# Sliding windows copied by DMA alone: 84 groups of 16 blocks through SBUF instead of 88, and direct copies of 32 rows instead of 16

## The chip, the core and the metric

The kernel runs on one core of a Trainium2 chip. No compute engine does any work in it: the data is moved by the core's 16 DMA engines, which are fed from two queues. SyncE (SP) issues the DMAs of one queue, ScalarE (ACT) those of the other. The metric is the device time of one execution in microseconds. Before the change the median of five runs is 760.02 us (757.92 to 760.73). The profile is of one execution that took 760.15 us.

## The reference

```python
x = randn(32, 4096, 256) float32           # batch, length, dim
window_size, stride = 64, 32
n_windows = (4096 - 64) // 32 + 1          # 127
for i in range(n_windows):
    result[:, i] = x[:, i * 32 : i * 32 + 64]
```

Nothing is computed; rows are copied. The length is cut into 128 blocks of 32 rows by 256 floats, 32 KB a block. Window i of a batch is blocks i and i+1, 64 KB in one piece, both in the input and in the output. Every block but the first and the last of a batch therefore lands in the output twice: as the first half of window i and as the second half of window i-1. The input has 134.2 MB, the output 266.3 MB.

## The kernel before

The batches are divided between two ways of copying, and the two run side by side from the first microsecond.

*Direct* (class `Direct`, issued by SP, line 45): batches 0 to 20. A DMA copies windows from the input in HBM to the output in HBM. A row of such a DMA is one window, 64 KB; the input is read at a step of one block, so that it is read twice over. The 127 windows of a batch take seven DMAs of 16 rows and one of 15. The argument `max_dma_last_dim` cuts a row into pieces: four of 16 KB in the DMAs of 16 rows, two of 32 KB in the DMA of 15 rows. That makes 147 DMAs of 16 rows (1024 KB) and 21 of 15 rows (960 KB). SP waits for nothing before it issues one.

*Staged* (class `Staged`, issued by ACT): batches 21 to 31. A group is 16 neighbouring blocks of a batch, 8 groups a batch, 88 in all. A group is loaded to SBUF once (line 79, 16 rows of 32 KB, cut in two pieces of 16 KB) and stored twice (line 91): once as first halves of windows (`half` 0), once as second halves (`half` 1). The first group of a batch has no second half for its first block, and the last group no first half for its last block, so that 22 of the 176 stores have 15 rows. There are 24 slots in SBUF for groups (6 tiles with 4 slots each). ACT loads 10 groups first (`LEAD`), and then in turn a group ten ahead and the two stores of a group. A store waits for its own load (`loaded`), a load into a slot that has been used waits for the two stores that read it (`stored`).

The order in each queue is thus the program's order. A DMA's pieces are given to the 16 engines by rows, and each engine that takes part ends its share of the DMA with a small write of 4 bytes that counts up a semaphore. Each engine has both queues before it. Every direct DMA and the stores of the last 24 groups count on the semaphore `done`, and SP waits for its full count at the end.

Of the kernel before, what the change touches and what calls it, by code (L numbers as in the profile page):

```python
# [1 line left out]

# [4 lines left out]


DIRECT, STAGE = 16384, 16384
N_STAGED = 11  # L10
N_TILES = 6
LEAD = 10


class Geometry:


    def __init__(self, tc, x, out, B, L, D, W, S, n_win):
        assert W == 2 * S and L % S == 0 and n_win == L // S - 1
        self.x, self.out = x, out  # L20
        self.blk, self.nb, self.nw = S * D, L // S, n_win
        self.done, self.total = tc.alloc_semaphore("done"), 0

    def xap(self, b, block, dims):
        return bass.AP(self.x.tensor, self.x.offset + (b * self.nb + block) * self.blk, dims)

    def oap(self, b, w, half, dims):
        at = ((b * self.nw + w) * 2 + half) * self.blk
        return bass.AP(self.out.tensor, self.out.offset + at, dims)

    def count(self, dma):
        dma.then_inc(self.done, 16)
        self.total += 16


class Direct:


    def __init__(self, g, batches):
        self.g, self.batches = g, batches  # L40

    def windows(self, q, b, w0, n, size):
        g = self.g
        g.count(
            q.dma_start(
                out=g.oap(b, w0, 0, [[2 * g.blk, n], [1, 2 * g.blk]]),
                in_=g.xap(b, w0, [[g.blk, n], [1, 2 * g.blk]]),
                max_dma_last_dim=size,
            )
        )  # L50

    def run(self, q):
        full = self.g.nw // 16 * 16
        for b in self.batches:
            for w0 in range(0, full, 16):
                self.windows(q, b, w0, 16, DIRECT)
            self.windows(q, b, full, self.g.nw - full, 2 * DIRECT)


class Staged:  # L60

    def __init__(self, g, tc, pool, dtype, batches, n_tiles):
        self.g = g
        tiles = [pool.tile([128, g.blk], dtype, name=f"xb{i}") for i in range(n_tiles)]
        self.slots = [t[32 + c : 96 : 4, :] for t in tiles for c in range(4)]
        self.loaded = [tc.alloc_semaphore(f"loaded{i}") for i in range(len(self.slots))]  # L70
        self.stored = [tc.alloc_semaphore(f"stored{i}") for i in range(len(self.slots))]
        self.groups = [(b, j) for b in batches for j in range(0, g.nb, 16)]

    def load(self, q, r):
        g, (b, j) = self.g, self.groups[r]
        n, i = divmod(r, len(self.slots))
        if n:
            q.wait_ge(self.stored[i], 32 * n)
        q.dma_start(
            out=self.slots[i], in_=g.xap(b, j, [[g.blk, 16], [1, g.blk]]),  # L80
            max_dma_last_dim=STAGE,
        ).then_inc(self.loaded[i], 16)

    def store(self, q, r):
        g, (b, j) = self.g, self.groups[r]
        n, i = divmod(r, len(self.slots))
        q.wait_ge(self.loaded[i], 16 * (n + 1))
        for half in (0, 1):
            lo = 1 if half and j == 0 else 0
            hi = 15 if not half and j + 16 == g.nb else 16  # L90
            dma = q.dma_start(
                out=g.oap(b, j + lo - half, half, [[2 * g.blk, hi - lo], [1, g.blk]]),
                in_=self.slots[i][lo:hi, :],
                max_dma_last_dim=STAGE,
            )
            if r + len(self.slots) < len(self.groups):
                dma.then_inc(self.stored[i], 16)
            else:
                g.count(dma)

    def run(self, q, lead):
        for r in range(lead):
            self.load(q, r)
        for r in range(len(self.groups)):
            if r + lead < len(self.groups):
                self.load(q, r + lead)
            self.store(q, r)


@with_exitstack  # L110
def kernel(
    ctx: ExitStack,
    tc: tile.TileContext,
    x: bass.AP,
    window_size: bass.AP,
    stride: bass.AP,
    out: bass.AP,
):
    nc = tc.nc
    W, S = int(window_size), int(stride)  # L120
    B, L, D = x.shape
    n_win = (L - W) // S + 1
    assert out.shape == (B, n_win, W, D)
    g = Geometry(tc, x, out, B, L, D, W, S, n_win)
    pool = ctx.enter_context(tc.tile_pool(name="xb", bufs=1))
    staged = Staged(g, tc, pool, x.dtype, range(B - N_STAGED, B), N_TILES)
    direct = Direct(g, range(B - N_STAGED))
    with tc.tile_critical():
        staged.run(nc.scalar, LEAD)
        direct.run(nc.sync)  # L130
        nc.sync.wait_ge(g.done, g.total)


# [1 line left out]
_INS = ['x', 'window_size', 'stride']  # L135
_OUTS = [((32, 127, 64, 256), 'float32')]

_NUMBERS = {'window_size': 64, 'stride': 32}


# [26 lines left out]
```

## Time and profile before

| what | value |
|---|---|
| median of five runs | 760.02 us (757.92 to 760.73) |
| the profiled execution | 760.15 us |
| its span, from the first to the last instruction | 758.4 us |
| busy compute engines | POOL 0.2 us, none else |
| bytes moved by the DMA engines | 312.53 MB, mean 412 GB/s |
| direct queue (q1, issued by SP) | 12705 packets, 174.80 MB |
| staged queue (q10, issued by ACT) | 12606 packets, 137.71 MB |
| last direct issue begins | 684.8 us |
| last store issue begins | 693.6 us |

A packet is one piece that one DMA engine moves: 16 KB, 32 KB or the 4 bytes of a semaphore. The span is to be read against the DMA rows only. The page's chain that ended last follows instructions of the compute engines, and there are none here. An issue that takes several microseconds is one that had to wait until the queue took it. "Us to landing" is from the issue of a DMA to the arrival of its last byte, and holds the time that it stood in its queue.

### The profile page before, as it was taken

To read this page: it belongs to the slowest core of one execution; us is meant where nothing else is said; L and a number is where in the kernel's file an instruction comes from. 1 tells how busy PE (TensorE), PEld (TensorE's weight loads), DVE (VectorE), ACT (ScalarE), POOL (GpSimd) and SP (SyncE) were. 2 spreads that over 40 slices of the span, in tenths; PEclk is the share of its full clock that TensorE was granted. 3 is DMA by queue.
4 is the path that set the end of the run, shared out by engine and by line. 5 is a ranking of instruction groups with operands and counts; after the bars stand their busy time and mean duration, and the time that the engine had idled before them with its cause. 6 is when DMAs were issued, how large, how long until landed. Compare 5 with 4: busy or idle time off the path is not lost. (4 is left out here: it accounts for less than half of the span.)

```text
span 758.4 us, 482 instructions
## 1 busy us (share of the span) xinstructions
POOL 0.2 (0%) x4
## 2 busy tenths in 40 slices
POOL 0000000000000000000000000000000000000000
DMA  8999999999999999999999999999999999999994
GB/s 365 417 404 412 417 423 418 418 426 419 424 418 425 419 421 423 420 425 420 422 412 427 422 418 418 425 421 423 421 424 413 424 416 423 417 422 414 404 403 200
DMA packets 25314, 312.53 MB, mean 412 GB/s; under 512 B 6869, under 2 KB 6869, under 8 KB 6869
## 3 DMA queue, kind: packets, MB, share of 16 engines
q1 hardware_dynamic: 12705, 174.80, 55.1%
q10 hardware_dynamic: 12606, 137.71, 43.6%
q14 instruction: 3, 0.02, 0.0%
HBM read 220.92 MB, written 266.34 MB: 643 GB/s over the span
## 5 line engine op out<-in xcount | busy, mean ns | idle before, releaser
L148 POOL MEMSET const-bfloat16-1.0<- 128x1 bf16 x1 | 0.1, 101 | 0.0
L148 POOL MEMSET const-uint8-127<- 128x1 uint8 x1 | 0.1, 101 | 0.0
L148 POOL MEMSET const-float32-0.0<- 128x1 f32 x1 | 0.1, 98 | 0.2 <-issue 0.2
L148 POOL MEMSET const-float32-1.0<- 128x1 f32 x1 | 0.1, 98 | 0.0
## 6 DMA issues: line engine op xcount, KB each, us to landing
out_dram<-in_x_dram SPq DMA_DIRECT2D x147, 1024.0 KB, 70.4
out_dram<-xb ACTq DMA_DIRECT2D x154, 512.0 KB, 69.5
xb<-in_x_dram ACTq DMA_DIRECT2D x88, 512.0 KB, 72.3
out_dram<-in_x_dram SPq DMA_DIRECT2D x21, 960.0 KB, 69.6
out_dram<-xb ACTq DMA_DIRECT2D x22, 480.0 KB, 69.8
```

Of the source, the lines that this page charges most:

```text
L148: nc = _bacc.Bacc("TRN2", target_bir_lowering=False, num_devices=1)
```

## The change

Two constants take the place of one: `GROUPS = 84` for `N_STAGED = 11`, and a new `ROWS = 32`. The staged part is now the last 84 groups of all 256: the second half of batch 21 (blocks 64 to 127) and batches 22 to 31. The direct part is everything before: batches 0 to 20, and windows 0 to 63 of batch 21. Direct DMAs take 32 rows as long as 32 are left, then 16, then the rest. A batch of 127 windows takes three DMAs of 32 rows, one of 16 and one of 15; the 64 windows of batch 21 take two of 32. The very first staged group leaves out the second half of its first block, because window 63 is now copied directly.

```diff
-N_STAGED = 11
+GROUPS = 84
+ROWS = 32
@@ class Direct
-    def __init__(self, g, batches):
-        self.g, self.batches = g, batches
+    def __init__(self, g, windows):
+        self.g = g
+        self.parts = [(b, min(g.nw, windows - b * g.nw)) for b in range(-(-windows // g.nw))]
...
     def run(self, q):
-        full = self.g.nw // 16 * 16
-        for b in self.batches:
-            for w0 in range(0, full, 16):
-                self.windows(q, b, w0, 16, DIRECT)
-            self.windows(q, b, full, self.g.nw - full, 2 * DIRECT)
+        for b, n in self.parts:
+            w0 = 0
+            while n - w0 >= 16:
+                m = ROWS if n - w0 >= ROWS else 16
+                self.windows(q, b, w0, m, DIRECT)
+                w0 += m
+            if n > w0:
+                self.windows(q, b, w0, n - w0, 2 * DIRECT)
@@ class Staged
-        self.groups = [(b, j) for b in batches for j in range(0, g.nb, 16)]
+        self.groups = groups
...
-            lo = 1 if half and j == 0 else 0
+            lo = 1 if half and (r == 0 or j == 0) else 0
@@ tile_sliding_window_1d_kernel
-    staged = Staged(g, tc, pool, x.dtype, range(B - N_STAGED, B), N_TILES)
-    direct = Direct(g, range(B - N_STAGED))
+    groups = [(b, j) for b in range(B) for j in range(0, g.nb, 16)][-GROUPS:]
+    staged = Staged(g, tc, pool, x.dtype, groups, N_TILES)
+    b, j = groups[0]
+    direct = Direct(g, b * g.nw + j)
```

More of the change, by code (lines that the diff above doesn't have):

```diff
@@ L52, in run, with __init__ @@
     def run(self, q):
-        full = self.g.nw // 16 * 16
-        for b in self.batches:
-            for w0 in range(0, full, 16):
-                self.windows(q, b, w0, 16, DIRECT)
-            self.windows(q, b, full, self.g.nw - full, 2 * DIRECT)
+        for b, n in self.parts:
[6 more added lines that the diff above has]
+                self.windows(q, b, w0, n - w0, 2 * DIRECT)
 class Staged:
-    def __init__(self, g, tc, pool, dtype, batches, n_tiles):
+    def __init__(self, g, tc, pool, dtype, groups, n_tiles):
         self.g = g
```

## The prediction

> **What bounds the kernel now.** I read the page's DMA rows first, since no compute engine works, then the stretches of the span with their DMA share, then the instructions in order of time, and last the packet records in the trace. The page:
>
> ```profile
> DMA packets 25314, 312.53 MB, mean 412 GB/s; under 512 B 6869, under 2 KB 6869, under 8 KB 6869
> ## 3 DMA queue, kind: packets, MB, share of 16 engines
> q1 hardware_dynamic: 12705, 174.80, 55.1%
> q10 hardware_dynamic: 12606, 137.71, 43.6%
> ...
> HBM read 220.92 MB, written 266.34 MB: 643 GB/s over the span
> ...
> out_dram<-in_x_dram SPq DMA_DIRECT2D x147, 1024.0 KB, 70.4
> out_dram<-xb ACTq DMA_DIRECT2D x154, 512.0 KB, 69.5
> xb<-in_x_dram ACTq DMA_DIRECT2D x88, 512.0 KB, 72.3
> out_dram<-in_x_dram SPq DMA_DIRECT2D x21, 960.0 KB, 69.6
> out_dram<-xb ACTq DMA_DIRECT2D x22, 480.0 KB, 69.8
> ```
>
> The two queues' shares add up to 98.7%: the 16 DMA engines are the bound, and what counts is the list of the most loaded one. The packet counts give it. A 16-row direct DMA is 64 pieces and 16 semaphore writes, a 15-row one 30 pieces and 15 writes: 147 x 80 + 21 x 45 = 12705, as shown. For the staged queue, (88 + 154) x 48 + 22 x 45 = 12606, as shown. So a row goes to an engine whole, and a 15-row DMA leaves one engine out. In units of 16 KB, 15 engines have 147 x 4 + 21 x 4 = 672 direct and 88 x 2 + 176 x 2 = 528 staged, 1200 together; the sixteenth has 588 + 484 = 1072.
>
> The stretches (start:end, length, POOL's busy time, clock, DMA share, GB/s):
>
> ```profile
> 20.00:200.00 180.00, 0.00 (x0) 1.00 1.01 418
> 200.00:400.00 200.00, 0.00 (x0) 1.00 1.01 421
> 400.00:600.00 200.00, 0.00 (x0) 1.00 1.01 421
> 600.00:690.00 90.00, 0.00 (x0) 1.00 1.01 420
> 690.00:700.00 10.00, 0.00 (x0) 1.00 0.97 411
> 700.00:740.00 40.00, 0.00 (x0) 1.00 0.95 404
> 740.00:744.00 4.00, 0.00 (x0) 1.00 0.98 418
> 744.00:748.00 4.00, 0.00 (x0) 1.00 0.72 307
> 748.00:752.00 4.00, 0.00 (x0) 1.00 0.31 131
> ```
>
> From 20 to 690 us all engines are full (packets overlap by some 4 ns, hence 1.01). From 700 on one is done: 15/16 is 0.94. Between 744 and 756 the other 15 end one by one, each at its own pace, and the slowest sets the time. A second reading: 421 GB/s over 16 engines is 26.3 each, 404 over 15 is 26.9. While all 16 run, the engines lose 2.3% to stalls that are gone in the drain. The packet records say the same: a 16 KB packet takes 611 ns undisturbed (most do), 624 on average before 690 us and 611 after it; a semaphore write takes 9 ns.
>
> ```profile
> 593.98 97.46 SPq L45 DMA_DIRECT2D out_dram<-in_x_dram  x21
> ...
> 623.48 70.69 ACTq L91 DMA_DIRECT2D out_dram<-xb  x22
> ```
>
> SP issues until 691.4 us, ACT until 694.2. Both queues are full to the end and run dry together. They hold nearly equal numbers of packets but 27% different bytes, so an engine takes one packet from each in turn, a semaphore write counting as a turn. In the records, neighbouring packets of an engine come from different queues in 97 of 100 cases.
>
> **The change part by part.**
>
> *Four groups leave the staged part.* That takes 4 loads and 8 stores from ACT, 2 units each on every engine: 24 units. Their 64 windows come back as four times 16 rows, 4 units each: 16. The slot waits and the lead of 10 groups stay: a group holds 9 packets on an engine, some 70 packets stand in a queue (a DMA takes 70 us to landing at one queue packet per 0.95 us), so a load is 8 groups in the queue and 10 ahead. That margin counts packets and does not move.
>
> *Direct DMAs of 32 rows.* Two windows an engine, 8 units and one semaphore write instead of 8 and two. The direct list becomes 65 DMAs of 32 rows, 21 of 16, 21 of 15: 520 + 84 + 84 = 688 units. The staged list is 84 loads and 168 stores, 22 of these still with 15 rows (10 batch starts, 11 ends, the new first group): 504 units. Together 1192, 8 fewer than 1200. One unit is (55.1% + 43.6%) x 758.4 = 748.5 us over the mean list of 1192 units: 0.628 us, of which 0.003 is semaphores. 8 x 0.625 = **-5.0 us**.
>
> *Semaphore writes.* 168 + 264 = 432 a loaded engine now, 107 + 252 = 359 after; 73 x (9 - 4) ns = **-0.3 us**. Fewer issues on SP and ACT cost or save nothing: both wait for room in a full queue (70 us behind).
>
> *The turns.* Packets of a loaded engine before: direct 588 + 42 + 168 = 798, staged 528 + 264 = 792. The packet records show the direct queue alone for the last 4.2 us on those engines, six packets over. After: 604 + 42 + 107 = 753 and 504 + 252 = 756. Still level, three packets over on the staged side, and the lone direct end still ran at 611 ns a packet: **0**. Had only the groups been moved, the direct queue would have 818 packets against 756; the longer DMAs take that away again.
>
> [...]
>
> *Stalls.* They cost 2.3% of 690 us, 16 us. What makes them the trace does not show. Lower end: they stop when the last DMAs are issued, so they may go with the issues; 107 + 252 = 359 DMAs instead of 432 is -17%, -2.7 us. Upper end: they may go with HBM traffic. Direct bytes touch HBM twice, staged bytes once, so traffic is engine rate x (1 + direct share): 431 GB/s undisturbed x 1.559 = 672 before, and with 178.98 MB direct of 310.38 in all, x 1.577 = 680 after. In the drain 404 x 1.56 = 630 ran without stalls. 16 us over 42 GB/s makes +3.0 us for 8 more. The nearest row is the middle of the span, the same state at almost the same mix, which says 0; the change of mix is towards more traffic, so I go a third of the way up: **+1.0 us**.
>
> Sum: -5.0 - 0.3 + 0 + 1.0 = -4.3 us on a span of 758.4, 754.1. The profiled execution took 760.15 and the median is 760.02, so I count from the median: **755.7 us**.
>
> **The rivals.** *A: two rows an engine make the direct packets stall (slower).* Which rows an engine gets is not in the trace; if two neighbours, the 16 engines write at steps of 128 KB instead of 64 KB. For it: stalls exist, and the direct packets of 32 KB, another form, lose 54 ns each, 27 per 16 KB, against 13.6 of those of 16 KB. If the 520 two-row units stalled like that: 520 x 13.5 ns = +7.0 us, 762.7 us. It decides from 4.3 / 520 = 8 ns a packet on. Against it: 85% of the packets run at the floor, and engines drift apart by microseconds, so they don't step together.
>
> [...]
>
> *B: the stalls go with the issues:* -2.7 instead of +1.0, 752.0 us. For it: they end within some microseconds of the last issue. Against: the sixteenth engine and the last load end there too.
>
> *C: the queues run dry apart.* If an engine gave time rather than turns, shares would stay 672 : 528 and the staged queue would end when the direct one has 688 - 641 = 47 units left, 28 us alone. If HBM gives no more than the 656 GB/s of the middle (421 x 1.559), direct alone moves 328 GB/s and these take 9 us longer: 765 us. The alternating packets speak against it. That 32 rows are not dealt out two to each engine would cost far more (one engine with three rows: 65 x 4 x 0.61 = 159 us); rows of 16 and 15 are dealt evenly.
>
> **How the numbers follow.** Forecast with stalls between -1.5 and +3.0: 0.68. B: 0.10. A: 0.18, of which a third lands near no change. C and uneven rows: 0.04. No change is within 0.2%, 758.5 to 761.5, about what a measurement of this kernel can tell. Faster 0.76 (forecast and B, less 0.02 for stalls beyond +3), same 0.08, slower 0.16. The likeliest case alone has 753 to 758; down to 751.5 it takes in B less the spread of the runs, up to 761.5 the milder half of A.
>
> **What would show it.** Right: 11985 and 12030 packets in the two queues, 178.98 and 131.40 MB, HBM read 223.0 MB; 107 issues on SP; the middle of the span at 418 to 422 GB/s; both queues' issues ending within some microseconds of each other near 685 us. A shows as a middle below 416 GB/s, B as one above 423, C as a long last stretch with one queue alone and one issue end well before the other. I would be wrong above all if the stalls, 16 us that I can't explain, are steep in something the change moves.

## The result, and the profile after

The changed kernel takes 761.72 us (median of 27 runs, 759.74 to 764.89) against 759.98 us for the kernel before (48 runs). The ratio is 1.0025, 95% interval 1.0015 to 1.0034: slower by a quarter of a per cent. The forecast was 4.3 us faster. The measured median lies 0.2 us above the end of the range.

The change did what it says. The page of the changed kernel (queue: packets, MB, share of 16 engines; then the traffic to HBM and the longer issues):

```profile
q1 hardware_dynamic: 11985, 178.99, 56.9%
q10 hardware_dynamic: 12030, 131.42, 42.0%
...
HBM read 223.02 MB, written 266.34 MB: 644 GB/s over the span
...
out_dram<-in_x_dram SPq DMA_DIRECT2D x65, 2048.0 KB, 81.3
```

Packets, bytes and HBM reads are those that were worked out, to the last packet. The queues also share the engines as foreseen: by the packet records the two run out 1.2 us apart on each of the 15 loaded engines. What went wrong is the pace. Stretches of the changed kernel (start:end, length, POOL's busy time, clock, DMA share, GB/s):

```profile
200.00:400.00 200.00, 0.00 (x0) 1.00 1.01 416
400.00:600.00 200.00, 0.00 (x0) 1.00 1.01 415
600.00:690.00 90.00, 0.00 (x0) 1.00 1.00 416
690.00:700.00 10.00, 0.00 (x0) 1.00 0.97 416
700.00:740.00 40.00, 0.00 (x0) 1.00 0.94 402
748.00:752.00 4.00, 0.00 (x0) 1.00 0.67 287
```

Before, the middle ran at 421 GB/s; now at 415 to 416. The DMA share is 1.01 in both, so the share shows nothing. The drain from 700 us on has not altered (404 and 402). The packet records give the same: an average 16 KB packet takes 631 ns instead of 624, on the direct queue and on the staged one alike. I call stall what a packet takes beyond its undisturbed time (611 ns for 16 KB, 1213 for 32 KB, and 309 for the 8 KB of some runs below: the medians in the records); summed and divided by 16 it is 16.7 us an engine before and 24.6 after. That is +7.9 us against a list that is 5.3 us shorter: +2.6 us on the average engine. The profiled spans differ by 1.5 us and the medians by 1.7.

### The profile page after: what moved, and what is told of

Read it like the earlier page. It is cut to its first block, busy times and chain, and to the rows that moved or that the text cites. A ratio compares the mean times of both kernels' runs of the same rounds, so it can differ in the third digit from the quotient of the medians.

```text
span 759.9 us, 409 instructions
## 1 busy us (share of the span) xinstructions
POOL 0.2 (0%) x4
## 3 DMA queue, kind: packets, MB, share of 16 engines
HBM read 223.02 MB, written 266.34 MB: 644 GB/s over the span
```

## Experiments

Every ratio below is against runs of the kernel before on the same chip, whose median is between 760.0 and 763.7 us in these sets. The diffs are against the changed kernel where they take GROUPS or ROWS away, else against the kernel before, if nothing else is said. The question is what the stalls follow. Theory MIX: the direct share of the bytes, because a direct byte touches HBM twice and a staged one once (in the page of the kernel before, twice 174.80 MB and 137.71 are 487.3, as are the 220.92 read and 266.34 written). Its rivals: two neighbouring rows on an engine (STEPS, rival A of the prediction), or the longer list of packets per DMA (LISTS). Later texts call the idea of MIX, put as a limit on HBM traffic, CAP or TRAFFIC, and the view of the prediction, that the engines' lists set the time, ENGINES.

**The mix of the changed kernel without its 32-row DMAs.**

```diff
-ROWS = 32
+ROWS = 16
...
-                self.windows(q, b, w0, m, DIRECT)
+                k += 1                      # every fifth or so: 31 of 151
+                self.windows(q, b, w0, m, 2 * DIRECT if k * 31 // 151 > (k - 1) * 31 // 151 else DIRECT)
```

> 84 groups as in the changed kernel, but direct DMAs of 16 rows throughout, 31 of the 151 cut in 32 KB pieces instead of 16 KB so that the direct queue has 756 packets a loaded engine, as many as the staged one. The list of a loaded engine (1192 units of 16 KB) and the bytes that each queue moves per turn are those of the changed kernel; no engine has two rows of a DMA. Theory MIX (stalls follow the direct share of the bytes in flight, through HBM traffic): the middle of the span at 415 GB/s as in the changed kernel, time near 761.5 us. Theory STEPS (two neighbouring rows on an engine make the engines' addresses 128 KB apart, and that stalls): the middle at 420 GB/s, near 755 us. Theory LISTS (a longer list of packets per DMA in a queue stalls): also 420 GB/s and 755 us.

Measured: 764.94 against 762.12 us, ratio 1.0037 (1.0015 to 1.0058). Its middle:

```profile
200.00:400.00 200.00, 0.00 (x0) 1.00 1.01 414
400.00:600.00 200.00, 0.00 (x0) 1.00 1.01 413
```

As slow as the changed kernel, with no engine getting two rows and no longer list than before. MIX is right here, the two rivals are not. The 32 KB pieces are not the cause by themselves: the 16 KB packets take 631 ns on the direct queue and 633 on the staged one, as in the changed kernel.

**The 32-row DMAs with the mix of the kernel before.**

```diff
-GROUPS = 84
+GROUPS = 88
...
-                self.windows(q, b, w0, m, DIRECT)
+                k += m == ROWS              # 7 of 63
+                self.windows(q, b, w0, m, DIRECT // 2 if m == ROWS and k % 9 == 0 else DIRECT)
```

> 88 groups as in the kernel before, direct DMAs of 32 rows as in the changed kernel, 7 of the 63 cut in 8 KB pieces so that the direct queue has 791 packets a loaded engine against 792. The list of a loaded engine is 1200 units and the bytes per turn are those of the kernel before. MIX: the middle at 421 GB/s, 760 us. STEPS and LISTS: the middle at 415 GB/s or less, 767 us.

Measured: 764.26 us, ratio 1.0020 (1.0002 to 1.0038).

**The kernel before with every second window in a DMA.**

```diff
...
-            for w0 in range(0, full, 16):
-                self.windows(q, b, w0, 16, DIRECT)
+            for w0 in range(0, full // 32 * 32, 32):
+                self.windows(q, b, w0, 16, DIRECT, 2)      # step of two windows
+                self.windows(q, b, w0 + 1, 16, DIRECT, 2)
+            self.windows(q, b, full - 16, 16, DIRECT)
```

> The kernel before, with one thing altered: six of the seven 16-row direct DMAs of a batch take every second window (even ones of 32, then odd ones), so that the rows of a DMA stand 128 KB apart in the output and 64 KB in the input. Lists, turns and counts are unchanged. MIX and LISTS: 760 us, the middle at 421 GB/s. STEPS: the middle at 415 GB/s, 768 us.

Measured: 763.98 us, ratio 1.0015 (0.9997 to 1.0032). The middles of these two, the first of the 32-row kernel:

```profile
200.00:400.00 200.00, 0.00 (x0) 1.00 1.01 419
400.00:600.00 200.00, 0.00 (x0) 1.00 1.01 417
```

and of the kernel with every second window:

```profile
200.00:400.00 200.00, 0.00 (x0) 1.00 1.01 418
400.00:600.00 200.00, 0.00 (x0) 1.00 1.01 418
```

The run with the groups alone, below, has the middle of the kernel before on this chip: 419 to 420. STEPS asked for 415 GB/s and 767 to 768 us in both, LISTS in the first; neither came. Both kernels may be a microsecond or two slower than before, at the edge of what the intervals tell; so a small part for the rows' addresses stays open. With rows 128 KB apart in the output the kernel is at most 0.3% slower (1.0015, interval to 1.0032).

**The groups alone.**

```diff
-ROWS = 32
+ROWS = 16
```

> The changed kernel with 16-row direct DMAs: the groups alone are moved. 1192 units, 818 direct packets a loaded engine against 756 staged. The middle should run as before (421 GB/s) under every theory, since turns and bytes per turn are those of the kernel before; some 62 direct packets, 52 units, are then left alone at the end, about 32 us of work. MIX: direct alone is held by HBM (656 GB/s of traffic at most, 328 GB/s of copies) and takes 10 us longer, 764 us. STEPS and LISTS: the lone stretch runs at full rate, 755 us.

Measured: 765.62 us, ratio 1.0041 (1.0022 to 1.0060). Its stretches:

```profile
200.00:400.00 200.00, 0.00 (x0) 1.00 1.01 420
400.00:600.00 200.00, 0.00 (x0) 1.00 1.01 419
...
700.00:720.00 20.00, 0.00 (x0) 1.00 1.00 392
720.00:740.00 20.00, 0.00 (x0) 1.00 0.95 328
```

The middle is that of before, since the turns are. Then the direct queue is alone and copies at 328 GB/s with the engines 95% "busy". 328 GB/s read and 328 written is 656 GB/s of HBM traffic; in the middle 421 x 1.559 is 656 as well. The lone direct packets at 611 ns that the prediction saw at the end of the kernel before came while the other engines still took turns or had finished; with all or nearly all of them in it, the direct queue alone doesn't run at that pace (its 16 KB packets take 757 ns on average between 722 and 738 us).

**The longer DMAs alone.**

```diff
-GROUPS = 84
+GROUPS = 88
```

> The changed kernel with 88 groups: the longer direct DMAs alone. 1200 units as before; 735 direct packets a loaded engine against 792, so that in the middle the direct queue has the share of the changed kernel (0.578) and the staged queue is left alone at the end with 38 units. TRAFFIC: the middle at 413 to 415 GB/s, stalls 6 to 8 us more than before, no HBM limit in the lone end: 6 to 7 us slower than before. If the stalls came of the groups moved: the middle as before, time as before.

Measured: 769.99 against 762.83 us, ratio 1.0088 (1.0061 to 1.0115). Its middle:

```profile
200.00:400.00 200.00, 0.00 (x0) 1.00 1.01 414
400.00:600.00 200.00, 0.00 (x0) 1.00 1.01 413
```

A semaphore write counts as a turn: in the records of the kernel before, neighbouring packets of an engine, semaphore writes among them, come from different queues in 97 of 100 cases. Fewer of them in the direct queue (its page has 11697 packets there, against 12705) give it more bytes per turn, and the middle falls to 413 or 414 though not a byte was moved from one part to the other: 7 us lost. So it is the 32-row DMAs that bring the stalls, by raising the direct share of the bytes in flight (0.578 of them in the middle by the packet records, against 0.557 in the kernel before); moving the groups gives 5.3 us of list back.

**The unchanged copies.** The kernel before, for its trace on the chip of the next three runs, and the changed kernel once more, on the chip of the run with the longer DMAs alone:

> The kernel before, unaltered, for its trace on the chip of the three runs beside it. Theory CAP: the middle of the span stands at some 650 to 655 GB/s of HBM traffic (copy rate times one plus the direct share), 418 to 420 GB/s of copies, whatever the engines' busy share says. Theory ENGINES (the engines' lists bound it, and stalls are an addition of a few per cent): the same row, it tells nothing apart by itself.

> The changed kernel, unaltered, beside the three others on one chip: the middle at 413 to 415 GB/s, 1.5 to 3 us slower than before.

The first has 417 to 419 GB/s in its three long stretches to 600 us and 19.2 us of stalls; its middle:

```profile
200.00:400.00 200.00, 0.00 (x0) 1.00 1.01 419
400.00:600.00 200.00, 0.00 (x0) 1.00 1.01 419
```

The second has 763.87 us, ratio 1.0010 (0.9989 to 1.0031), 413 to 414 GB/s and 26.8 us of stalls. The ratio agrees with that of the result within its interval, which takes in no change as well.

**The other way: more groups.**

```diff
-GROUPS = 84
-ROWS = 32
+GROUPS = 96                 # 92 and 104 in the others
+ROWS = 16
...
+                small = k * few // of > (k - 1) * few // of    # 26 of 140; 12 of 144; 53 of 133
+                self.windows(q, b, w0, m, DIRECT // 2 if small else DIRECT)
```

> The other way: 92 groups staged, direct DMAs of 16 rows, 12 of 144 cut in 8 KB pieces so that both queues have 828 packets a loaded engine. A loaded engine has 656 + 552 = 1208 units, 8 more than before; direct share of the bytes 0.542, HBM traffic of the whole 485.2 MB against 487.3. CAP: copies in the middle at 655 / 1.542 = 425 GB/s; 291.2 MB outside the drain instead of 289.1 at 420: about 2.5 us faster than before. ENGINES: 5 us slower.

> 96 groups staged, 26 of 140 16-row direct DMAs in 8 KB pieces, 864 packets a loaded engine in each queue. 640 + 576 = 1216 units, direct share 0.528, HBM traffic 483.1 MB. CAP: the middle at 655 / 1.528 = 429 GB/s, just under the engines' 431; about 4 us faster than before, less if the two limits round each other off. ENGINES: 10 us slower.

> 104 groups staged, 53 of 133 16-row direct DMAs in 8 KB pieces, 934 and 936 packets a loaded engine. 608 + 624 = 1232 units, direct share 0.493. CAP: HBM would allow 439 GB/s, the engines allow 431, so that they are the bound and packets of 16 KB run near 611 ns in the middle; about 2 us slower than before and 6 slower than with 96 groups. ENGINES: 20 us slower than before.

Measured, against 761.94 us: 92 groups 763.46 us, ratio 1.0013 (0.9993 to 1.0032); 96 groups 762.52 us, 1.0010 (0.9997 to 1.0024); 104 groups 766.91 us, 1.0073 (1.0050 to 1.0096). The middle with 96 groups:

```profile
200.00:400.00 200.00, 0.00 (x0) 1.00 1.01 425
400.00:600.00 200.00, 0.00 (x0) 1.00 1.01 426
```

and with 104:

```profile
200.00:400.00 200.00, 0.00 (x0) 1.00 1.01 429
400.00:600.00 200.00, 0.00 (x0) 1.00 1.01 427
```

ENGINES asked for 5, 10 and 20 us more, where 1.5, 0.6 and 5.0 came by the medians, and falls. CAP foresaw the middle with 104 groups nearly free of stalls, which it is, but promised 2.5 and 4 us of gain with 92 and 96, which did not come. The limit is not sharp: stalls are 5.1 us with 104 groups, 10.0 with 96, 15.3 with 92, 19.2 with 88 and 26.8 with 84 (the last on the chip of the second copy). Every four groups fewer take 5 us off the list. From 104 to 96, eight groups, that is 10 us off and 5 of stalls on; then 5.3, 3.9 and 7.6 us of stalls come on for 5 off. From 88 to 96 groups the time is flat within the intervals, and at 84 the stalls outweigh the list.

**Traffic or something else about direct copies?** One seventh of the 16-row direct DMAs read a piece of SBUF, filled once, instead of the input. Those windows get other data.

```diff
+                self.k += 1
+                if self.k % EVERY:          # EVERY = 7
                     self.windows(q, b, w0, 16, DIRECT)
+                else:                       # the same list and writes, 1 MB of HBM reads fewer
+                    self.filled(q, b, w0, 16)
```

> The kernel before with one seventh of the 16-row direct DMAs (one a batch, 21 in all) reading from a piece of SBUF that is filled once at the start, in place of the input; those windows get other data. Lists (1200 units), turns, pieces and the bytes written to HBM are unchanged; HBM reads fall by 22 MB, HBM traffic from 487.3 to 465.3 MB, 1.489 for each byte copied, which is what the kernel with 104 groups has (1.493). Theory TRAFFIC (stalls follow the HBM traffic that the engines ask for): the middle at 427 to 429 GB/s as there, stalls down from 19 to some 5 us an engine, 746 to 750 us where the kernel before has 762 on such a chip. If the stalls come of something else in the direct copies or in the staged ones: the middle at 418 to 420, time as before.

Measured: 789.34 against 762.83 us, ratio 1.0306 (1.0265 to 1.0347), neither theory's time. The page's row of GB/s in 40 slices:

```profile
GB/s 318 424 280 421 334 422 337 431 372 426 390 419 398 422 411 421 416 417 411 416 412 421 417 411 425 422 422 414 424 422 427 423 423 423 425 411 404 385 348 102
```

Slices of 421 to 431 alternate with holes. The source lay in 16 neighbouring partitions. Of the 16 KB packets, 126 of the direct queue take over 2 us, against 6 of the staged queue, whose stores read partitions four apart. The run had measured its own source, as the next one shows. What makes neighbouring partitions slow as a source no run here shows. The next run differs from this one in the source: a spare slot, 16 partitions four apart, so that 23 slots are left for the groups.

```diff
+        self.spare = self.slots.pop()       # t[32 + 3 : 96 : 4, :] of the last tile; 23 slots stay
...
-        direct.prepare(nc.sync, tc, staged.tiles[0])      # its partitions 0 to 15
+        direct.prepare(nc.sync, tc, staged.spare)
```

> As the run with SBUF sources before it, but the piece of SBUF is a spare slot, 16 partitions four apart, as the staged stores read them (23 slots are left for the groups). One seventh of the 16-row direct DMAs get other data; lists of 1200 units and turns as in the kernel before, HBM traffic 465.3 MB instead of 487.3. TRAFFIC: the middle at 427 to 429 GB/s, stalls near 5 us an engine instead of 19, 12 to 16 us faster than before. If the stalls come with the direct copies themselves or with the staged ones: the middle at 418 to 420, time within 3 us of before.

Measured: 752.16 against 763.74 us, ratio 0.9860 (0.9830 to 0.9890); 8.4 us of stalls. Its page and stretches:

```profile
q1 hardware_dynamic: 12753, 175.32, 55.2%
q10 hardware_dynamic: 12606, 137.71, 43.6%
...
HBM read 199.43 MB, written 266.34 MB: 621 GB/s over the span
```

```profile
200.00:400.00 200.00, 0.00 (x0) 1.00 1.01 428
400.00:600.00 200.00, 0.00 (x0) 1.00 1.01 425
```

The lists of the engines, the turns, the pieces and the writes are those of the kernel before, but for one fill at the start. Only reads from HBM are fewer, and the stalls fall by 11 us against the copy of the kernel before, the time by 11.6. The staged queue, which has the same work in both, shows it too: its 16 KB packets take 618 ns on average, against 627 in that copy. So the stalls come of something that both queues share, and TRAFFIC is shown; the gain is a little under the 12 to 16 us expected. Whether it is reads, writes or their sum that is limited, this run doesn't tell; the next one does.

**The limit by itself.** All batches direct, nothing staged:

```diff
...
-    direct = Direct(g, range(B - N_STAGED))
+    direct = Direct(g, range(B))
...
-        staged.run(nc.scalar, LEAD)
```

> All 32 batches direct, nothing staged: 1024 units a loaded engine, which at 0.607 us would be 622 us; HBM traffic 532.7 MB. TRAFFIC: at 650 to 655 GB/s it takes 815 to 820 us, copies at 326 GB/s throughout, with the engines' busy share still near 1. ENGINES: near 640 us.

Measured in one execution: 821.47 us. Its page and middle:

```profile
q1 hardware_dynamic: 19360, 266.35, 98.4%
...
HBM read 266.34 MB, written 266.34 MB: 650 GB/s over the span
```

```profile
200.00:400.00 200.00, 0.00 (x0) 1.00 1.00 329
400.00:600.00 200.00, 0.00 (x0) 1.00 1.00 327
```

The engines have 15% fewer units than before and are "busy" 98.4% of the span, and the kernel is 8% slower. 327 to 329 GB/s of copies are 654 to 658 of traffic. The middle of the kernel before has some 298 GB/s of reads and 359 of writes (421 times the page's 220.92 and 266.34 MB over 312.53); here it is 328 of each. Neither alone stands at the same value in both, their sum does.

**A shorter list at the same traffic.** 96 groups, and the last 15 windows of 16 batches joined:

```diff
+            if b == JOINT - 1:              # JOINT = 16; 30 of 140 DMAs in 8 KB pieces
...
+                for half in (0, 1):         # 16 batches x 15 half windows of 32 KB, a batch an engine
...
+                    out=g.oap(0, w0, half, [[g.nw * 2 * g.blk, JOINT], [2 * g.blk, n], [1, g.blk]])
+                    in_=g.xap(0, w0 + half, [[g.nb * g.blk, JOINT], [g.blk, n], [1, g.blk]])
```

> 96 groups staged as tried, with the last 15 windows of batches 0 to 15 copied by two joint DMAs after batch 15 (one for the first halves of the windows, one for the second, a batch to each engine) instead of sixteen DMAs of 15 rows: all 16 engines have 60 units there, where 15 had 64. A loaded engine's list falls from 1216 to 1212 units at the same HBM traffic and equal packets in both queues (864). If the engines' list counts at this mix: 2.4 us faster than with 96 groups before, which is 0.2% faster than the kernel before. If HBM alone counts, or the joint DMAs' steps of 4 MB in the input and 8 MB in the output stall: no gain, or a loss in the stretch after batch 15.

Measured: 772.42 us, ratio 1.0125 (1.0096 to 1.0155). The page's row of GB/s:

```profile
GB/s 361 409 421 422 415 428 425 430 427 428 430 424 426 430 432 428 431 428 429 429 426 431 430 429 430 425 432 428 382 321 330 336 425 427 428 430 422 419 405 252
```

Four slices at 321 to 382, where the joint DMAs pass, lack 347 of 4 x 429 GB/s, some 16 us at 19.2 us a slice. The run lost 9 us against the first one with 96 groups; elsewhere it is faster (429 GB/s from 200 to 400 us, against 425), with the 15-row DMAs gone from the mix up to there and fewer direct bytes in flight. What the list alone is worth at this mix was not answered. The joint packets of 32 KB come with the 16 engines 4 MB apart in the input and 8 MB in the output, and with a larger direct share for that while. The share alone doesn't make the holes: between 565 and 615 us the packet records have 72% direct bytes at 328 GB/s, which is 566 GB/s of traffic, well below the 650 and more of the other runs. So it is something of the joint DMAs themselves, their addresses perhaps; that was not shown apart. No version that writes the right windows was faster than the kernel before in these runs.

## Why the prediction was wrong

Step by step, as the prediction put it:

- *Four groups leave, 1200 to 1192 units, -5.0 us, and semaphore writes -0.3 us:* right in the counts (page above; 73 x 5 ns is 0.37). That the list counts at its full price shows between the longer DMAs alone (1.0088) and the changed kernel on the same chip (1.0010): 6 us by medians for those four groups at nearly the same middle.
- *The turns, 0:* right as to their evenness. But the same paragraph held the loss: that the longer DMAs need fewer turns is what raises the direct share in flight. The prediction carried this into its stalls (x 1.577 for x 1.559) and priced it far too low there.
- *Stalls, between -2.7 and +3.0, taken as +1.0:* this is the step that failed. They measured +7.9 us (+7.6 between the two copies, on two other chips). The upper end had the right cause, HBM traffic, and a wrong curve: a straight line from no stalls at 630 GB/s to 16 us at a demand of 672, which is 0.38 us for each GB/s. The five group counts, with demands of 643, 658, 665, 672 and 680 GB/s (431 times one plus the direct share), have 5.1, 10.0, 15.3, 19.2 and 26.8 us: near that line up to 658, and from 672 to 680 almost 1 us for each GB/s. The row "nearest" by state, the middle of the span, was the worst to lean on, since that state already stood at the limit. At the limit the size can be worked out: 656 GB/s over 1.559 is 421 and over 1.577 is 416, 1.1% less, and 1.1% of 690 us is 8 us.
- *What bounds the kernel:* "the 16 DMA engines are the bound", read off 98.7% busy, is half right. A packet that waits for HBM counts as busy; all-direct shows 98.4% at 327 GB/s. The middle stood at 421 x 1.559 = 656 GB/s of traffic, after the change at 416 x 1.577 = 656 again, and all-direct at 654 to 658: the same ceiling. The prediction had this number in rival C and did not use it for the middle. The change adds 0.43% of traffic (489.4 MB for 487.3); over the 690 us at the ceiling that is +3 us, against 1.7 measured. The same sum is no forecast for every mix: with 92 and 96 groups it promised gains that did not come.
- *Rival A, two rows an engine, +7 us of stalls:* its size came true, which is luck, and its mechanism did not. The same stalls came without two rows (1.0037), and two rows at the old mix cost 1.0020.
- *Rival B, stalls go with issues:* no. Issues fell by 17% and stalls rose by half.
- *Rival C, direct alone at 328 GB/s:* did not happen here, since the turns were even; but its pace, worked out from the ceiling, was met when the groups were moved alone (328 GB/s).

## What to carry to other kernels

A busy share of DMA engines near 1 does not tell engine time from waiting for memory (98.7% at a mean of 412 GB/s before, 98.4% at 325 all direct): set the copied bytes beside the traffic they cause, and find the rate at which traffic stops growing, best with a run that has nothing but the costlier kind. Where two queues take turns packet by packet, fewer packets in one queue also shift the mix in flight (a direct share of 0.578 for 0.557 here), and a kernel that stands where two limits meet gives back on the one what it gains on the other (7.9 us of stalls for 5.3 us of list). An experiment that swaps a source should keep the source's layout, or it measures that (789.34 us with neighbouring partitions, 752.16 with partitions four apart).

## What the runs showed of the hardware

- In these runs HBM traffic of the one core, reads and writes together, levels off at 650 to 658 GB/s, whether direct copies are all of the bytes (329 GB/s copied) or 56% (421).
- Stalls set in below that: 104 groups ask for 431 x 1.493 = 643 GB/s and have 5.1 us of them.
- Direct DMAs of 16 rows that read 16 neighbouring SBUF partitions make holes down to 280 GB/s in a 20 us slice; with partitions four apart the same DMAs leave none below 396 between the first slice and the last.
- Rows 4 MB apart in the source and 8 MB in the destination, one to an engine, went with 321 to 336 GB/s where 429 stood before, at 566 GB/s of traffic (565 to 615 us).
